# Newton steps with one operand in PSUM, and a gated half normalised by two engines, in a two-layer mixer block on one Trainium2 core

## The chip, the cores and the metric

The kernel runs on one core of one Trainium2 chip, as one launch. The metric is the device time of an execution in microseconds (us). The names used throughout are those of the profile: PE is TensorE, DVE is VectorE, ACT is ScalarE, POOL is GpSimd and SP is SyncE, which issues the loads. PSUM is the memory that PE writes its results to; SBUF is the large on-chip memory that every engine works from.

## The reference

Two layers over 512 tokens (`x`) and 256 context tokens (`ctx`), 1024 features, float32. Layer 0 mixes tokens with a gated MLP over chunks of 128 tokens beside a differential attention of four heads; layer 1 with a sliding-window attention with sinks, for the 512 tokens alone. Each layer ends with a SwiGLU feed-forward of width 2816, and a last root-mean-square norm follows.

```python
def rmsnorm(x, g):
    y = x * rsqrt(mean(x * x, axis=-1) + EPS)
    return y * g

def modulate(x, g, shift, scale):
    return rmsnorm(x, g) * (1 + scale) + shift

def chunk_mlp(u, v, w_s, b_s):          # the gated half
    u, vf = gelu(u), gelu(v)            # split in chunks of 128 tokens and 4 groups of 128 features
    mu = mean(vf, axis=-1)
    vf = (vf - mu) * rsqrt(mean((vf - mu)**2, axis=-1) + EPS)
    mixed = einsum('gpq,bnqgc->bnpgc', w_s, vf) + b_s
    return u * mixed

def diff_attn(q, k, v, lam):
    p = softmax(q @ k * scale)          # two maps for each head
    return (p[0] - lam * p[1]) @ v

# layer 0: y = concat(chunk_mlp(u, v), rmsnorm(diff_attn(q, k, vv), subln_g) * (1 - lam_init)) @ w_out
```

## The kernel before

Activations are kept feature-major: a tile has 128 features on the partitions, and 512 + 256 = 768 tokens in its columns. A float32 product is made of three matmuls on halves (`mm3`, L99, L100, L101): each operand is split into a rounded half (a cast on ACT, L115 or L75) and a rest (a subtraction on DVE or POOL: `split` L116, `unit` L78 for weights).

The program is written with tiles and a scheduler. Before anything runs, the scheduler simulates the engines and sets the order of the instructions on each one, by priorities and its simulated times; the pools of tiles decide which instruction must wait for a buffer. On the chip each engine then works through its list in that order. A stage may be pulled ahead of others by `tc.high_priority`. PSUM has three kinds of buffers here: `bank()` (three, tag `pb` in the profile), `fill()` (one, `pf`) and `wide()` (two, `pw`).

A norm over features goes like this. `squares` gathers squares; `rstd_diag` (L138 to L171) takes them with a ones matrix (L149, more terms L153) into a bank, so that each token's sum of squares stands in a column per block of 128 tokens. L156 (or L158 in the heads, with an epsilon for each token) scales the sums and adds epsilon, from PSUM into a small SBUF tile of 2 to 6 columns (`sm`). `rsqrt_small` (L123 to L133) makes the reciprocal root: a seed on the bits (L128), and three Newton steps of three instructions each (L130, L131, L132), all in SBUF on DVE. L165 writes one diagonal matrix for each block (`ident` times the root); `spread` multiplies it with ones on PE (L175), which puts the root of each token on all partitions. Fourteen such norms are in the kernel: before the mixers and the feed-forwards, one for each of the four heads of layer 0, and the last one. `rstd_small`, used for the gated half, calls the same `rsqrt_small` on 24 columns (`sf`).

The order around the change in layer 0 is: `head(0)` to `head(3)` (attention; scores into `wide()`, maximum L534, exponential, difference L542, transposes L554 into a bank, split, product with the values into another bank). `norm(t-1, …)` for the head before is called inside `head(t)`; for the last head it follows behind it. Beside the heads PE has the input products of the gated MLP (`gated`, into `fill()`), and for each of four groups `turn` (transposes L634, copy, statistics on DVE). Then `rs = rstd_small(...)` and `mix(g, rs)` for g = 0 to 3: on a group's six blocks, in two halves of four and two, L648 normalises a block in place on DVE (subtract the mean `mv[:, t, 0:1]`, multiply by the root), L649 multiplies it with the 128 x 128 chunk matrix into `pw = self.fill()`, and L650 evacuates the half and adds the bias. L677 multiplies by the other, gelu-activated half, and a split (L115, L116) prepares the operand of the output projection, whose eight weight slabs are loaded, cast (L75) and subtracted (L78) beside it. The slabs are used in the order heads 0, 1, 2, groups 0 to 3, head 3; the rests of the second and third head's operands (`k in (5, 6)`) are made by POOL's L116.

Of the kernel before, what the change touches and what calls it, by code (L numbers as in the profile page):

```python
# [6 lines left out]
F32 = mybir.dt.float32  # L7
F32R = mybir.dt.float32r
BF16 = mybir.dt.bfloat16
I32 = mybir.dt.int32  # L10
AF = mybir.ActivationFunctionType
ALU = mybir.AluOpType
AX = mybir.AxisListType.X

P = 128
# [11 lines left out]
class Builder:  # L27
# [96 lines left out]
    def rsqrt_small(self, v, n, tag="sm", bufs=6):  # L124
# [7 lines left out]
            ve.scalar_tensor_tensor(y, t, 1.5, y, ALU.add, ALU.mult)  # L132
        return y  # L133

    def rstd_rows(self, acc, T, inv, bank=None, dg=None, more=(), out=None):
        return self.spread(self.rstd_diag([(acc, T)], inv, bank, None, dg, more)[0], out or bank)

    def rstd_diag(self, accs, inv, bank=None, eps=None, at=None, more=()):  # L138

        nc = self.nc  # L140
        nb = sum(T for _, T in accs) // P
        ms = self.small(nb)
        o = 0
        for acc, T in accs:
            ps = (bank or self.bank)()
            n = T // P
            for j in range(n):
                c = slice(j * P, (j + 1) * P)
                nc.tensor.matmul(ps[:, c], acc[:, c], self.ones, start=j == 0, stop=not more, skip_group_check=True)  # L149
            for t in more:  # L150
                for j in range(n):
                    c = slice(j * P, (j + 1) * P)
                    nc.tensor.matmul(ps[:, c], t[:, c], self.ones, start=False, stop=t is more[-1], skip_group_check=True)  # L153
            col = ps[:, 0:T].rearrange("p (j f) -> p j f", f=P)[:, :, 0]
            if eps is None:
                nc.vector.tensor_scalar(ms[:, o:o + n], col, inv, EPS, ALU.mult, ALU.add)  # L156
            else:
                nc.vector.scalar_tensor_tensor(ms[:, o:o + n], col, inv, eps[:, o:o + n], ALU.mult, ALU.add)  # L158
            o += n
        r = self.rsqrt_small(ms, nb)  # L160
        dgs, o = [], 0
        for acc, T in accs:
            dg = at if at is not None else self.tmp()
            for j in range(T // P):
                self.last_diag = nc.vector.tensor_scalar(dg[:, j * P:(j + 1) * P], self.ident, r[:, o + j:o + j + 1], None,  # L165
                                                         ALU.mult)
            dgs.append(dg[:, :T])
            o += T // P
        return dgs
# [142 lines left out]
    def even(self):  # L312
        tc, nc, a = self.tc, self.nc, self.a
# [13 lines left out]
        for k in range(0, KT, 2):  # L327
            t = self.load(Rh, a["xT"][k * P:(k + 2) * P, :].rearrange("(k p) t -> p k t", p=P), [P, 2, TX], f"hx{k}")
# [110 lines left out]
        for half, heads in enumerate(((0, 1), (2, 3))):  # L439
# [3 lines left out]
            for k in range(KT):  # L443
                t = self.adap.tile([P, 2, 512], F32R, name=self.uid("wq"), tag="wq", bufs=3) if k % 3 == 2 else None
# [8 lines left out]
                if half == 0:  # L453
                    t, sh = hx[k], self.modcol(0, 0, k, 0)
# [29 lines left out]
        Rv = tc.alloc_tile_pool(name="v0", bufs=1, side="right", reuse_waits="tile")  # L484
# [5 lines left out]
        for k in range(KT):  # L490
            W = self.unit(a["v0"][k * P:(k + 1) * P, :], 512)
            for tb in range(6):
                c = slice(tb * P, (tb + 1) * P)
# [74 lines left out]
        def gated(i):  # L568

            W = self.blocks(a["uv"][i])  # L570
            u = f3()
            for off, T, A in ((0, TX, axx), (TX, TC, axc)):
                ps = self.fill()[:, :T]
                self.dense(ps, W, A)
                nc.scalar.copy(u[:, off:off + T], ps)
            raw[i] = u
# [49 lines left out]
        mv = Rv.tile([P, 24, 2], F32, name="mv")  # L626
# [14 lines left out]
        def mix(g, rs):  # L641

            vg = raw[4 + g]
            for off, n in halves:
                pw = self.fill()
                for i in range(n):
                    s, t = slice((off + i) * P, (off + i + 1) * P), g * 6 + off + i
                    nc.vector.tensor_scalar(vg[:, s], vg[:, s], mv[:, t, 0:1], rs[:, t:t + 1], ALU.subtract, ALU.mult)  # L648
                    nc.tensor.matmul(pw[:, i * P:(i + 1) * P], vg[:, s], sguT[:, g * P:(g + 1) * P], start=True, stop=True)  # L649
                nc.vector.tensor_tensor(vg[:, off * P:(off + n) * P].rearrange("p (n q) -> p n q", q=P),  # L650
                                        pw[:, :n * P].rearrange("p (n q) -> p n q", q=P),
                                        sgub[:, g * P:(g + 1) * P].unsqueeze(1).to_broadcast([P, n, P]), ALU.add)
# [13 lines left out]
        for g in range(4):  # L666
            turn(g)
            gated(g)
        rs = self.rstd_small(mv[:, :, 1], 24, 1.0, "sf")
        for g in range(4):  # L670
            mix(g, rs)
        cat = {}
# [708 lines left out]
```

## Time and profile before

| quantity | value |
|---|---|
| median of three runs | 1652.94 us (1651.64 to 1657.9) |
| profiled execution | 1665.51 us, of which the span 1663.7 |
| busy in the span | PE 1547.9, DVE 1079.5, POOL 811.8, ACT 720.6 us |
| mean granted clock of PE | 0.97 |

The span is the time from the first to the last instruction that the profile holds. Times in the timeline are counted from its start. A line of the timeline gives the start, the duration from the start of the first to the end of the last of a run of equal instructions, engine, line, operation, the tile written and those read, shapes, the number of instructions, and in brackets the idle time of the engine before it with what ended it. Layer 0's heads run from about 180 to 325 us, the turn to its output projection lies around 320 to 350, layer 1's first norm at 973, and the last norm from 1643.

### The profile page before, as it was taken

To read this page: it belongs to the slowest core of one execution; us is meant where nothing else is said; L and a number is where in the kernel's file an instruction comes from. 1 tells how busy PE (TensorE), PEld (TensorE's weight loads), DVE (VectorE), ACT (ScalarE), POOL (GpSimd) and SP (SyncE) were. 2 spreads that over 40 slices of the span, in tenths; PEclk is the share of its full clock that TensorE was granted. 3 is DMA by queue.
4 is the path that set the end of the run, shared out by engine and by line. 5 is a ranking of instruction groups with operands and counts; after the bars stand their busy time and mean duration, and the time that the engine had idled before them with its cause. 6 is when DMAs were issued, how large, how long until landed. Compare 5 with 4: busy or idle time off the path is not lost.

```text
span 1663.7 us, 24643 instructions
## 1 busy us (share of the span) xinstructions
PE 1547.9 (93%) x9547; PEld 1372.0 (82%) x9547; DVE 1079.5 (65%) x1953; ACT 720.6 (43%) x1460; POOL 811.8 (49%) x581
## 2 busy tenths in 40 slices
PE   6999989989889998999999988999989899999996
PEld 4776867889878898999999978777869889898886
DVE  4622787855666888666667585665667756566665
ACT  2413665633443332333333244556665444444443
POOL 0562211050666756766676415532224766666662
PEclk9999989989999999999999999999999999999998
DMA  8754100123122424343342012110233132223201
GB/s 313 296 173 148 33 7 1 64 79 125 51 77 89 139 90 139 118 149 136 132 144 95 26 50 83 58 33 20 77 120 116 55 111 89 102 77 114 89 26 51
DMA packets 47957, 161.98 MB, mean 97 GB/s; under 512 B 5472, under 2 KB 9952, under 8 KB 40160
## 3 DMA queue, kind: packets, MB, share of 16 engines
q1 hardware_dynamic: 47696, 160.28, 28.1%
q8 instruction: 75, 1.23, 0.3%
q14 instruction: 42, 0.34, 0.1%
q10 hardware_dynamic: 144, 0.13, 0.0%
HBM read 158.29 MB, written 2.10 MB: 96 GB/s over the span
## 4 chain that ended last, share of the span: by engine, by line
PE 70%; DVE 14%; ACT 4%; DMA 4%; POOL 3%; issue 3%; POOLq 0%; SPq 0%; DVEq 0%; ACTq 0%
PE pw L99 9%; PE pw L100 9%; PE pw L101 9%; PE pb L99 8%; PE pb L100 8%; PE pb L101 8%; DMA raw<-ffn_in 3%; POOL w L896 3%; PE pf L99 2%; PE pf L100 2%; PE pf L101 2%; PE pb L1234 2%; PE pb L1223 2%; DVE junk L220 2%; PE pf L349 2%
## 5 line engine op out<-in xcount | busy, mean ns | idle before, releaser
L99 PE MATMUL pw<-ax,w 128*128 128x384 f32 (+2 forms) x732 | 239.4, 331 | 22.8 <-DVE hs L929 6.6
L78 POOL TENSOR_TENSOR w<-raw,w 128x512 fp32r<-128x512 f32 (+1 forms) x84 | 127.8, 1528 | 249.3 <-ACT w L75 226.6
L100 PE MATMUL pw<-ax,w 128*128 128x384 f32 (+2 forms) x732 | 240.1, 328 | 4.0 <-DVE ax L193 2.6
L101 PE MATMUL pw<-ax,w 128*128 128x384 f32 (+2 forms) x732 | 238.3, 326 | 2.2 <-POOL w L896 2.2
L896 POOL TENSOR_TENSOR w<-raw,w 128x512 fp32r<-128x512 f32 x124 | 192.2, 1565 | 43.1 <-ACT w L893 43.1
L896 POOL TENSOR_TENSOR w<-t,w 128x512 fp32r<-128x512 f32 x92 | 133.0, 1445 | 143.7 <-ACT w L893 142.1
L99 PE MATMUL pb<-hh,w 128*128 128x512 f32 x480 | 168.0, 363 | 14.2 <-ACT hh L115 8.5
L99 PEld LDWEIGHTS pw<-ax,w 128*128 128x128 f32 x732 | 143.6, 197 | 34.7 <-DVE hs L929 6.9
L100 PE MATMUL pb<-hh,w 128*128 128x512 f32 x480 | 171.1, 357 | 0.0
L101 PE MATMUL pb<-hh,w 128*128 128x512 f32 x480 | 170.9, 357 | 0.0
L99 PE MATMUL pw<-T,w 128*128 128x384 f32 (+1 forms) x508 | 158.7, 312 | 9.3 <-DVE hs L929 4.7
L757 DVE SCALAR_TENSOR_TENSOR xT<-pb,mod,xT 128x512 f32<-128x512 f32 (+3 forms) x208 | 144.4, 703 | 26.0 <-PE pb L101 25.4
L100 PE MATMUL pw<-T,w 128*128 128x384 f32 (+1 forms) x508 | 157.8, 311 | 2.1 <-DVE T L116 1.5
L101 PE MATMUL pw<-T,w 128*128 128x384 f32 (+1 forms) x508 | 157.4, 310 | 0.0
L100 PEld LDWEIGHTS pw<-ax,w 128*128 128x128 f32 x732 | 144.4, 197 | 12.1 <-DVE ax L193 3.6
L101 PEld LDWEIGHTS pw<-ax,w 128*128 128x128 f32 x732 | 144.0, 197 | 6.1 <-POOL w L896 2.6
L893 ACT CAST w<-t 128x512 fp32r<-128x512 f32 x104 | 64.5, 621 | 184.1 <-DVE t L945 139.0
L99 PEld LDWEIGHTS pb<-hh,w 128*128 128x128 f32 x480 | 89.9, 190 | 28.6 <-ACT hh L115 10.9
L99 PEld LDWEIGHTS pw<-T,w 128*128 128x128 f32 x508 | 96.6, 190 | 14.2 <-DVE hs L929 5.2
L220 DVE SCALAR_TENSOR_TENSOR junk<-ar,cb 128x1024 bf16<-128x1024 f32 x64 | 106.7, 1667 | 0.2
L896 POOL TENSOR_TENSOR w<-rawo,w 128x512 fp32r<-128x512 f32 x66 | 95.2, 1443 | 19.7 <-ACT w L893 19.7
L101 PEld LDWEIGHTS pb<-hh,w 128*128 128x128 f32 x480 | 90.5, 188 | 13.1
(364 smaller groups left out, 4077.1 us busy)
## 6 DMA issues: line engine op xcount, KB each, us to landing
raw<-ffn_in SPq DMA_DIRECT2D x44, 1024.0 KB, 5.0
ar<-ada SPq DMA_DIRECT2D x24, 1024.0 KB, 6.9
ar<-ada SPq DMA_DIRECT2D x48, 512.0 KB, 3.8
rawo<-ffn_out SPq DMA_DIRECT2D x44, 512.0 KB, 3.8
raw<-odd_out SPq DMA_DIRECT2D x32, 256.0 KB, 2.7
raw<-qk SPq DMA_DIRECT2D x16, 256.0 KB, 7.6
raw<-uv SPq DMA_DIRECT2D x16, 256.0 KB, 2.7
raw<-even_out SPq DMA_DIRECT2D x8, 512.0 KB, 3.5
```

The source lines that it names most:

```text
L78: eng.tensor_tensor(lo, raw, hi.bitcast(F32), ALU.subtract)
L99: mm(out, s[0], m[0], start=start, stop=False, **kw)
L100: mm(out, s[0], m[1], start=False, stop=False, **kw)
L101: return mm(out, s[1], m[0], start=False, stop=stop, **kw)
L220: self.nc.vector.scalar_tensor_tensor(junk, t, 1.0, self.cb[who], ALU.mult, ALU.mult, accum_out=self.acc[who][:, col:col + 1])
L349: nc.tensor.matmul(ps[32 * q:32 * q + 32, :w], cst[:, k, :], t[:, w * q:w * q + w], start=k == 0, stop=k == KT - 1, skip_group_check=True)
L757: self.nc.vector.scalar_tensor_tensor(h, ps[:, r], self.modcol(l, j, m, who), h, ALU.mult, ALU.add)
L893: nc.scalar.copy(t[:, 0, :], src)
L896: eng.tensor_tensor(t[:, 1, :], src, t[:, 0, :].bitcast(F32), ALU.subtract)
L1223: last = nc.tensor.transpose(pt[:, x * P:(x + 1) * P], es[2 * (x % 2) + x // 2][:, kb * P:(kb + 1) * P], self.ident)
L1234: nc.tensor.matmul(po[64 * h:64 * h + 64, :], V[vb][:, 64 * g:64 * g + 64], t[:, h * TC:h * TC + TC], start=kb == 0, stop=kb == nb - 1, sk ...
```

## The change

Two things are changed.

*The Newton iteration* of the fourteen norms is `rsqrt_bank`. Beside the root `y` it carries the product `x` = v·y, so that in each round `tp` = -0.5·x·y is made from both, and y = (tp + 1.5)·y and x = (t + 1.5)·x follow, `t` being a second copy of `tp` in SBUF. The value v, `x` and `tp` lie in PSUM, in columns 16, 32 and 48 of the bank that held the first sums; y and `t` lie in SBUF. So each instruction has one operand in PSUM and at most one in SBUF. It takes 12 instructions behind the scaling, where there were 10. The bank stays in use until the last of them. Where a norm has two sets of sums, both scalings write to the first bank.

*The gated half.* Blocks with an odd number are normalised by ACT, as Identity with scale `rs` and bias `mb` = -mean·`rs` (a new 24-column tile, one DVE instruction), the others by DVE as before. The second half of each group (two blocks) is mixed into a `bank()`, the first (four) into `fill()` as before.

```diff
+    def rsqrt_bank(self, v, n, x, tp):
+        ve = self.nc.vector
+        y, t = self.small(n), self.small(n)
+        ve.tensor_scalar(y.bitcast(I32), v.bitcast(I32), -0.5, float(0x5F3759DF), ALU.mult, ALU.add)
+        ve.tensor_tensor(x, v, y, ALU.mult)
+        for i in range(3):
+            ve.scalar_tensor_tensor(tp, x, -0.5, y, ALU.mult, ALU.mult)
+            if i < 2:
+                ve.scalar_tensor_tensor(t, x, -0.5, y, ALU.mult, ALU.mult)
+                ve.scalar_tensor_tensor(x, t, 1.5, x, ALU.add, ALU.mult)
+            ve.scalar_tensor_tensor(y, tp, 1.5, y, ALU.add, ALU.mult)
+        return y
...
-        ms = self.small(nb)
         o = 0
         for acc, T in accs:
             ps = (bank or self.bank)()
+            if not o:
+                ms, *at2 = [ps[:, c:c + nb] for c in (16, 32, 48)]
...
-        r = self.rsqrt_small(ms, nb)
+        r = self.rsqrt_bank(ms, nb, *at2)
...
             for off, n in halves:
-                pw = self.fill()
+                pw = (self.bank if off else self.fill)()
                 for i in range(n):
                     s, t = slice((off + i) * P, (off + i + 1) * P), g * 6 + off + i
-                    nc.vector.tensor_scalar(vg[:, s], vg[:, s], mv[:, t, 0:1], rs[:, t:t + 1], ALU.subtract, ALU.mult)
+                    if i % 2:
+                        nc.scalar.activation(vg[:, s], vg[:, s], AF.Identity, bias=mb[:, t:t + 1], scale=rs[:, t:t + 1])
+                    else:
+                        nc.vector.tensor_scalar(vg[:, s], vg[:, s], mv[:, t, 0:1], rs[:, t:t + 1], ALU.subtract, ALU.mult)
...
         rs = self.rstd_small(mv[:, :, 1], 24, 1.0, "sf")
+        mb = Rv.tile([P, 24], F32, name="mb")
+        nc.vector.scalar_tensor_tensor(mb, mv[:, :, 0], -1.0, rs, ALU.mult, ALU.mult)
```

The scheduler's order moves with it. The rows below are the program's lists in order; the line numbers of after are its own (L174 is before's L158, L181 is L165, L191 is L175, L615 is L599, L668 is L649, L669 is L650, L698 is L677; L140 to L147 are the new steps).

DVE at the turn, before, from the normalisations (`f`) on; `sm` is the last head's norm, `pf_3129` and `pf_3139` are the first mixed halves:

```order
L648 TENSOR_SCALAR f_374_2099<-f_374_2099,mv,sf_3117 128x128 x6
L158 SCALAR_TENSOR_TENSOR sm_2738<-pb_2739,sx_2457 128x4
L116 TENSOR_TENSOR ax_3194<-o_1337,ax_3193 128x768
L128 TENSOR_SCALAR sm_2749<-sm_2738 128x6
L130 TENSOR_TENSOR sm_2750<-sm_2749 128x6
L131 SCALAR_TENSOR_TENSOR sm_2750<-sm_2750,sm_2738 128x6
L132 SCALAR_TENSOR_TENSOR sm_2749<-sm_2750,sm_2749 128x6
L650 TENSOR_TENSOR f_353_1910<-pf_3129,sgub_1297 128x512
...
L165 TENSOR_SCALAR q_2761<-ident_97,sm_2749 128x128 x4
L165 TENSOR_SCALAR q_2766<-ident_97,sm_2749 128x128 x2
L650 TENSOR_TENSOR f_360_1973<-pf_3145,sgub_1297 128x512
```

DVE at the same place, after:

```order
L690 SCALAR_TENSOR_TENSOR mb<-mv,sf_3123 128x24
L667 TENSOR_SCALAR f_371_2102<-f_371_2102,mv,sf_3123 128x128 x3
L174 SCALAR_TENSOR_TENSOR pb_2743<-pb_2743,sx_2461 128x4
L140 TENSOR_SCALAR sm_2753<-pb_2743 128x6
...
L147 SCALAR_TENSOR_TENSOR sm_2753<-pb_2743,sm_2753 128x6
L181 TENSOR_SCALAR q_2767<-ident_97,sm_2753 128x128 x4
L181 TENSOR_SCALAR q_2772<-ident_97,sm_2753 128x128 x2
L116 TENSOR_TENSOR ax_3202<-o_1339,ax_3201 128x768
L615 SCALAR_TENSOR_TENSOR o_2460<-o_2460,subg_1313,pb_2775 128x512
L615 SCALAR_TENSOR_TENSOR o_2460<-o_2460,subg_1313,pb_2778 128x256
L669 TENSOR_TENSOR f_350_1913<-pb_3147,sgub_1299 128x256
```

The new `mb` stands ahead of the normalisations. No evacuation of a mixed half stands within the norm any more: the first, L669, comes behind the norm's diagonals, an L116 and both L615, which read the spread roots `pb_2775` and `pb_2778`.

PE at the turn, before; `pw_3312` and its like are the output projection:

```order
L649 MATMUL pf_3129<-sguT_1295,f_353_1910 128x128 x4
L649 MATMUL pf_3139<-sguT_1295,f_353_1910 128x128 x2
L649 MATMUL pf_3145<-sguT_1295,f_360_1973 128x128 x4
L99 MATMUL pw_3312<-ax_3193,w_3256 128x384
L100 MATMUL pw_3312<-ax_3194,w_3256 128x384
L99 MATMUL pw_3313<-ax_3193,w_3256 128x384
L100 MATMUL pw_3313<-ax_3194,w_3256 128x384
L175 MATMUL pb_2769<-q_2761,ones 128x512
L175 MATMUL pb_2772<-q_2766,ones 128x256
L101 MATMUL pw_3312<-ax_3193,w_3256 128x384
```

After:

```order
L191 MATMUL pb_2775<-q_2767,ones 128x512
L191 MATMUL pb_2778<-q_2772,ones 128x256
L668 MATMUL pb_3147<-sguT_1297,f_350_1913 128x128 x2
L668 MATMUL pf_3137<-sguT_1297,f_350_1913 128x128 x4
L668 MATMUL pb_3163<-sguT_1297,f_357_1976 128x128 x2
L668 MATMUL pb_3179<-sguT_1297,f_364_2039 128x128 x2
L668 MATMUL pb_3195<-sguT_1297,f_371_2102 128x128 x2
L668 MATMUL pf_3153<-sguT_1297,f_357_1976 128x128 x4
L99 MATMUL pw_3320<-ax_3201,w_3264 128x384
L100 MATMUL pw_3320<-ax_3202,w_3264 128x384
```

PE had three halves to mix, four matmuls of the projection and then the spread of the last head's norm. Now the spread comes first, and six of the eight halves are mixed ahead of the projection, four of them in banks.

DVE in the second head, before, at the norm of the first head (`sm_1706`, `sm_1707`); `e` and `sa` are the attention's, `atl` the rests of its transposed maps:

```order
L132 SCALAR_TENSOR_TENSOR sm_1706<-sm_1707,sm_1706 128x6
L116 TENSOR_TENSOR atl_1779<-pb_1773,ath_1778 128x512
L534 TENSOR_REDUCE sa_1862<-pw_1870 128x1
L541 SCALAR_TENSOR_TENSOR sa_1857<-sa_1857,nlam,sa_1844 128x1
L130 TENSOR_TENSOR sm_1707<-sm_1706 128x6
L543 SCALAR_TENSOR_TENSOR sx_1601<-sa_1863 128x1
L542 SCALAR_TENSOR_TENSOR e_1849<-e_1855,sa_1857,e_1849 128x256
L116 TENSOR_TENSOR atl_1794<-pb_1788,ath_1793 128x512
L131 SCALAR_TENSOR_TENSOR sm_1707<-sm_1707,sm_1695 128x6
...
L132 SCALAR_TENSOR_TENSOR sm_1706<-sm_1707,sm_1706 128x6
L165 TENSOR_SCALAR q_1718<-ident_97,sm_1706 128x128 x4
```

After; `pb_1697` is the first bank of sums, in which the steps now work:

```order
L145 SCALAR_TENSOR_TENSOR sm_1708<-pb_1697,sm_1707 128x6
L116 TENSOR_TENSOR atl_1782<-pb_1776,ath_1781 128x512
L557 SCALAR_TENSOR_TENSOR sa_1860<-sa_1860,nlam,sa_1847 128x1
L146 SCALAR_TENSOR_TENSOR pb_1697<-sm_1708,pb_1697 128x6
L558 SCALAR_TENSOR_TENSOR e_1852<-e_1858,sa_1860,e_1852 128x256
L147 SCALAR_TENSOR_TENSOR sm_1707<-pb_1697,sm_1707 128x6
...
L147 SCALAR_TENSOR_TENSOR sm_1707<-pb_1697,sm_1707 128x6
L181 TENSOR_SCALAR q_1721<-ident_97,sm_1707 128x128 x4
L181 TENSOR_SCALAR q_1726<-ident_97,sm_1707 128x128 x2
...
L116 TENSOR_TENSOR atl_1797<-pb_1791,ath_1796 128x512
```

The second rest of that stretch, `atl_1794` before, stood between two Newton steps; its counterpart `atl_1797` now stands behind the norm's diagonals.

## The prediction

> **What bounds the kernel now.** I read the page first.
>
> ```profile
> span 1663.7 us, 24643 instructions
> PE 1547.9 (93%) x9547; PEld 1372.0 (82%) x9547; DVE 1079.5 (65%) x1953; ACT 720.6 (43%) x1460; POOL 811.8 (49%) x581
> PE 70%; DVE 14%; ACT 4%; DMA 4%; POOL 3%; issue 3%; POOLq 0%; SPq 0%; DVEq 0%; ACTq 0%
> ```
> TensorE (PE) is busy 93% of the span and holds 70% of the chain that ended last; VectorE (DVE) holds 14%. A stage is worth something to this change only where PE waits, so I went through the windows for stretches with PE holes, and from these into the timelines.
>
> ```profile
> 220.00:240.00 20.00, 15.72 (x109) 13.91 (x107) 17.69 (x49) 16.23 (x32) 2.58 (x2) 0.91 0.00 1
> 240.00:260.00 20.00, 16.41 (x71) 13.13 (x72) 14.94 (x37) 12.49 (x24) 1.81 (x1) 0.83 0.01 1
> 260.00:280.00 20.00, 17.25 (x109) 15.41 (x108) 18.04 (x56) 13.73 (x30) 4.60 (x3) 0.85 0.00 1
> 320.00:340.00 20.00, 12.22 (x72) 10.54 (x72) 18.76 (x49) 7.13 (x10) 8.74 (x4) 0.88 0.51 172
> ```
> Columns: PE, PEld, DVE, ACT, POOL busy, then the granted clock. From 320 to 340 us PE is busy 12.2 of 20 us: the turn from attention to the output projection, which the change edits. From 220 to 280, in the heads, PE loses 2.8 to 4.3 us per 20, DVE is busy up to 18 and the clock is at 0.83 to 0.91. The timeline of the turn, PE, DVE, then POOL:
>
> ```profile
> 325.47 1.50 PE L149 MATMUL pb<-ones,sq 128*128 128x128 f32 x12
> 330.29 1.16 PE L649 MATMUL pf<-sguT,f 128*128 128x128 f32 x8 [0.46 <-ACT f L575]
> 338.36 1.23 PE L649 MATMUL pf<-sguT,f 128*128 128x128 f32 x4 [6.91 <-DVE f L650]
> 322.39 6.24 DVE L648 TENSOR_SCALAR f<-f,mv,sf 128x128 f32<-128x128 f32 x24
> 329.56 1.79 DVE L128 TENSOR_SCALAR sm<-sm 128x6 int32<-128x6 int32 x1
> 331.39 1.72 DVE L130 TENSOR_TENSOR sm<-sm 128x6 f32<-128x6 f32 x1
> 333.15 2.26 DVE L131 SCALAR_TENSOR_TENSOR sm<-sm,sm 128x6 f32<-128x6 f32 x1
> 335.44 2.27 DVE L132 SCALAR_TENSOR_TENSOR sm<-sm,sm 128x6 f32<-128x6 f32 x1
> 337.63 0.68 DVE L650 TENSOR_TENSOR f<-pf,sgub 128x512 f32<-128x512 f32 x1
> 341.15 1.27 DVE L165 TENSOR_SCALAR q<-ident,sm 128x128 f32<-128x128 f32 x6
> 328.95 4.14 POOL L116 TENSOR_TENSOR ax<-o,ax 128x768 fp32r<-128x768 f32 x2 [55.79 <-ACT ax L115]
> 333.05 4.63 POOL L78 TENSOR_TENSOR w<-raw,w 128x1024 fp32r<-128x1024 f32 x2
> ```
> PE ran one group of mixing matmuls at 330.29 and stood still for 6.91 us, until DVE's evacuation L650, queued behind four Newton steps on a 128x6 tile. Each of these took 1.7 to 2.3 us and ended with one of POOL's four instructions (two L116, two L78, back to back to 337.68). All the same steps together:
>
> ```profile
> L130 DVE TENSOR_TENSOR sm<-sm x42: 143/161/1724, 14.4 to 1653.6; 128x2 f32<-128x2 f32 x18, 128x6 f32<-128x6 f32 x12, 128x4 f32<-128x4 f32 x6, 128x3 f32<-128x3 f32 x6
> L156 DVE TENSOR_SCALAR sm<-pb x5: 145/159/163, 14.0 to 1271.4; 128x2 f32<-128x2 f32 x3, 128x4 f32<-128x4 f32 x1, 128x3 f32<-128x3 f32 x1
> 354.80 0.68 DVE L650 TENSOR_TENSOR f<-pf,sgub 128x512 f32<-128x512 f32 x1
> 352.71 2.17 DVE L116 TENSOR_TENSOR ax<-f,ax 128x768 fp32r<-128x768 f32 x1 [0.90 <-ACT ax L115]
> 346.24 16.35 POOL L78 TENSOR_TENSOR w<-raw,w 128x1024 fp32r<-128x1024 f32 x6 [8.55 <-ACT w L75]
> 977.09 1.88 DVE L165 TENSOR_SCALAR q<-ident,sm 128x128 f32<-128x128 f32 x4
> ```
> A step takes 161 ns at the median and 1724 at most. L156 reads PSUM and never goes above 163 ns. While POOL ran L78 without a break from 346.24 to 362.6, L650 (one operand in PSUM) took 0.68 us, L116 (both in SBUF) 2.17. So DVE gives way to POOL when an instruction needs two SBUF reads, one DVE instruction per POOL instruction. The diagonal, L165 (ident, SBUF to SBUF), does too: four of them took 1.88 us at 977.09 as POOL's L78 began, while six took 1.27 at 341.15.
>
> **The change part by part.** The sum is made against the profiled execution: 1665.51 us, 1663.7 of span and 1.8 around it, 12.6 above the median of 1652.94; I shift by the difference.
>
> *Newton in a bank.* Every step now has one operand in PSUM and one in SBUF, so by the rows above it stops waiting for POOL. A norm has 13 short instructions for 11. Free of waits they start 0.20 us apart (337.63's neighbours and the first norm), so a norm is 0.4 us longer. No instruction of before writes PSUM from DVE; the nearest rows are the PSUM read at 159 ns and the SBUF step at 161. I take equal. The bad end is L156's own maximum of 163 ns against the minimum of L130, 143: 20 ns on each of 182 steps (13 in 14 norms), under 4 us if none lay beside other work; the good end is no difference. The Trainium skill ("Perfetto Trace Analysis", Optimizing Scalar/DVE Operations) speaks against the change here: it puts DVE's overhead per instruction at about 60 ns on SBUF and 125 on PSUM; by that a norm would be an estimated 0.8 us longer still (13 times 65 ns) and the sum some 3 us higher. The row of L156 disagrees for reads.
>
> *The turn.* Removed: four blocked steps. Moved: the evacuations L650 now stand behind the whole norm of the last head, its six diagonals, an L116 and two L599, and PE spreads the norm before it mixes. DVE's normalisations halve: 24 took 6.24 us from 322.39; 12 take 3.1, behind `mb` (0.2), to 325.7. ACT takes 12 from 322.6 on:
>
> ```profile
> L831 ACT ACTIVATE hh<-hh,mod 128x128 f32<-128x128 f32 x6 | 2.3, 390 | 0.0
> 325.72 0.58 ACT L575 COPY f<-pf 128x512 f32<-128x512 f32 x1 [4.55 <-PE pf L101]
> 327.25 2.30 ACT L115 CAST ax<-o 128x768 fp32r<-128x768 f32 x3 [0.94 <-PE pf L100]
> ```
> 390 ns each, and as ACT starts one 0.1 before the last ends (three casts of 0.83 took 2.30), 0.30 apart: 3.6 us, to 326.2. ACT's copy L575 then starts 0.5 us late, and PE, busy with L149 until 326.97, hides that but for 0.1. So DVE has the sums at 327.0, runs 13 steps and reaches the first diagonal at 329.6. POOL begins its four instructions after the second of ACT's casts L115, at 328.95, now 329.0. The diagonals are 0.6 us too late: I expect the block to move from the steps to them. One passes per POOL instruction; the fourth comes out with the last, near 337.3 (POOL's first is not held up by DVE's L116, 0.4 saved), the other two, L116 and the two L599 follow by 340.5. PE gets the spread at 337.4 instead of evacuated data at 338.36, and the clock decides the rest:
>
> ```profile
> 332.00:335.30 3.30, 0.00 (x0) 0.00 (x0) 3.27 (x2) 1.00 (x2) 3.30 (x2) 1.00 0.00 0
> 338.70:342.10 3.40, 2.88 (x13) 2.59 (x13) 2.69 (x11) 1.01 (x2) 0.00 (x0) 0.50 0.43 152
> 342.10:345.50 3.40, 3.40 (x10) 2.28 (x8) 2.08 (x5) 3.39 (x4) 0.00 (x0) 0.50 0.00 0
> 348.64 0.60 PE L649 MATMUL pf<-sguT,f 128*128 128x128 f32 x4
> 353.10 1.05 PE L649 MATMUL pf<-sguT,f 128*128 128x128 f32 x8
> ```
> The clock fell to 0.50 after a stretch without matmuls, and came back only after 3.4 us in which PE was busy throughout (2.88 of 3.40 wasn't enough). Before, PE entered the projection (P from here) at 345.46 with four of its matmuls done (0.7 us) and five mixing groups owed (28 matmuls; eight took 1.05 and four 0.60 at full clock, so each adds 0.11: 3.1): it would have ended both at 347.9 + P. With banks of both kinds PE has mixing for all of the recovery, so I expect full speed at 342.1 and the projection at 344.4 to 344.9 with two groups of eight owed (1.8): 346.2 to 346.7 + P. That is 1.2 to 1.7 earlier; I take **-1.4**. Bounds: +1 if the clock stays at half to 345.5, -10 if the block goes.
>
> *The heads.* Three norms run between the attention of the next head. DVE is the fullest engine there (18.04 of 20), so 2 x 0.2 x 3 = 1.2 us. And the first bank of sums, freed before by its first read, is held to the last step:
>
> ```profile
> 226.51 0.16 DVE L158 SCALAR_TENSOR_TENSOR sm<-pb,sx 128x4 f32<-128x4 f32 x1 [0.40 <-PE pb L149]
> 238.95 1.27 DVE L165 TENSOR_SCALAR q<-ident,sm 128x128 f32<-128x128 f32 x6
> ```
> Now it is held from 226.5 to the last step just ahead of 238.95, one bank of three, while the next head's transposes L554 need banks too. In the new order the second set of them comes behind the norm, and its cast on ACT (0.58 us for 512 columns, as L575 above) behind the gelus. I take **+1.8**: the three norms and one cast. Bounds: -1, since the order changes and PE has filler, and +11 (below).
>
> *The middle norm* (973 to 987) has a blocked L130 and L131 in the second half's chain, between modulations that PE waits for; two steps more in the first. The diagonal there ends with POOL's L78 anyway, which hides them. **-0.5**, from +0.4 to -1.5.
>
> *The last norm:*
>
> ```profile
> 1651.53 0.68 DVE L130 TENSOR_TENSOR sm<-sm 128x2 f32<-128x2 f32 x1
> 1654.29 0.65 DVE L131 SCALAR_TENSOR_TENSOR sm<-sm,sm 128x2 f32<-128x2 f32 x1
> 1655.16 0.48 DVE L165 TENSOR_SCALAR dg<-ident,sm 128x128 f32<-128x128 f32 x2
> 1650.78 4.14 POOL L1301 TENSOR_TENSOR xT<-xT,rs 128x256 f32<-128x256 f32 x6 [3.28 <-ACT rs L1291]
> 1655.70 1.22 PE L175 MATMUL pf<-dg,ones 128*128 128x256 f32 x2 [5.41 <-DVE dg L165]
> ```
> Five steps waited for POOL's six multiplications. Now 13 steps and L1303 take from 1649.8 to 1653.3; the half before is 0.4 later, since two more steps follow its last L757. The two diagonals wait for POOL once each: done by 1654.7 instead of 1655.6. Nothing hides PE's spread, so **-0.9** (0 to -1.5). The remaining norms lie under PE's work; if that cover were gone, 0.4 each for five, 2 us.
>
> Sum: -1.4 + 1.8 - 0.5 - 0.9 = -1.0 us. 1664.5 in a profiled run, 1652.0 by the median.
>
> **The rivals.** *Bank starvation, slower.* The held bank stalls the attention itself. Price: each of three holds delays a set of transposes by a cycle of transposes, cast and subtraction (0.6 for four matmuls, half of the eight's 1.16, then 0.58 and 0.68 as the rows of L575 and L650: 1.9 us) and starves PE long enough for one more 3.4 us at half clock (1.7): 3.6, three times 11; with the other terms, +8.5: 1661.5. It decides where PE has no filler (mixing inputs of L99) between the stalls. For: clock and holes of 240 to 260 above. Against: the filler is there, and the order puts it there.
>
> *The block goes, faster.* If the diagonals pass before POOL's run, PE's 6.9 us hole closes, and the half-clock work after it (2.88 + 3.40 us at half, 3.1 lost) with it: -10 in the turn; with +1.8, -0.5 and -0.9, -9.6: 1643.5. It needs 0.6 us: a Newton step faster than 0.15 us, or casts later by that. Against: steps have never been under 143 ns, and ACT's 12 delay the casts by 0.1 only. The Trainium skill ("SBUF — State Buffer", Who interferes with whom) has `tensor_scalar` able to take the shared ports in its two-port modes; by that the diagonals wait, as L165 at 977.09 does.
>
> *The change doesn't do what it says.* If steps with one operand in PSUM wait too (a write, not a read, taking the port), the last steps and then the diagonals are blocked: +2 in the turn, +1.5 at the end, about 1657. Against: L650 beside L116.
>
> **How the numbers follow.** Forecast 0.69, starvation 0.13, block gone 0.14, no effect 0.04. A measurement of this kernel can tell about 0.5% (8.3 us) from no change; the forecast's terms by themselves lie within that, as does the third rival. So faster 0.14, same 0.73, slower 0.13. The range reaches from the block gone, 1643.5, to 1661, just short of full starvation; the bounds of the single terms (one or two heads stalled, the clock late, the steps 20 ns longer) lie inside.
>
> **What would show it.** Right: the short steps in a bank stay near 0.16 us beside POOL, at 1650 too; six diagonals behind the last head's norm take 6 to 9 us, ended by POOL; PE's hole of 329.6 to 337 stays; the last diagonal ends near 1654.7. Wrong: diagonals of 1.3 us there and PE mixing by 332; PSUM steps above 0.2 us; new holes of PE with half clock in 225 to 310; the turn more than 3 us off in either direction.

## The result, and the profile after

The changed kernel takes 1661.39 us (median of 16 runs, 1657.06 to 1668.61) against 1654.3 us of the kernel before (16 runs, 1650.67 to 1657.9): ratio 1.0049, 95% interval 1.0036 to 1.0062: some 8 us slower by the ratio, 7.1 by the medians. The forecast was 1652 with a range to 1661.

The profiled execution of before that the prediction used (1665.51 us) was a long one, 11 us above its runs' median, while that of after (span 1659.8) is near its median. The two pages set side by side would show a gain. A second and a third profile of before have spans of 1653.4 and 1648.6 us; they are what after is compared with here. The head of the page of after:

```profile
span 1659.8 us, 24676 instructions
PE 1548.3 (93%) x9547; PEld 1373.4 (83%) x9547; DVE 1076.7 (65%) x1970; ACT 723.7 (44%) x1472; POOL 810.5 (49%) x581
PE 71%; DVE 12%; POOL 4%; ACT 4%; DMA 4%; issue 4%; POOLq 0%; SPq 0%; ACTq 0%; DVEq 0%
```
PE's share of the chain rose from 70 to 71%, POOL's from 3 to 4, DVE's fell from 14 to 12: averages that don't tell the place. So I cut each profile at the same matmuls. Stage times in us, worked out from the starts of matched matmuls in the timelines: *heads* from the first sums of the first head's norm to those of the last head's, *turn* from there to a matmul of the output projection (384 us), then the feed-forward of layer 0 to 960, layer 1's first norms and inputs to 1085, attention to 1190, attention's end, output projection, norms and the first products of the feed-forward to 1393 (*layer 1*), the rest to 1622, and *last* with the last norm (the bounds are named by their times in the second profile of before).

| profile | heads | turn | to 960 | to 1085 | to 1190 | layer 1 | to 1622 | last | span |
|---|---|---|---|---|---|---|---|---|---|
| before, second | 96.4 | 62.1 | 575.9 | 125.0 | 105.1 | 202.9 | 229.2 | 31.2 | 1653.4 |
| before, third | 96.6 | 62.2 | 574.2 | 124.3 | 105.1 | 200.3 | 228.9 | 31.2 | 1648.6 |
| before, first | 100.0 | 63.2 | 580.3 | 125.0 | 105.1 | 202.6 | 230.7 | 31.3 | 1663.7 |
| after | 103.5 | 59.9 | 575.6 | 123.1 | 105.1 | 207.4 | 230.4 | 30.0 | 1659.8 |
| after, second | 103.5 | 59.5 | 577.8 | 123.5 | 105.1 | 207.2 | 229.2 | 30.0 | 1662.6 |

The turn and the last norm gain 2.4 and 1.2 us. The heads lose 7 (3.5 against the one long profile of before), and layer 1 loses 4.4 to 7, in a stretch where the change touches two short norms. The stages to 960 and to 1622 vary by 2 to 6 us between profiles of one kernel; nothing is read from them.

**The turn.** The timeline of after, ACT, DVE, POOL, then PE (L665 is ACT's normalisation, L174 the scaled sums, L181 the diagonals, L191 the spread, L668 the mixing):

```profile
325.53 4.73 ACT L665 ACTIVATE f<-f,mb,sf 128x128 f32<-128x128 f32 x12 [1.43 <-DVE mb L690]
331.32 2.30 ACT L115 CAST ax<-o 128x768 fp32r<-128x768 f32 x3 [0.59 <-PE pf L100]
329.90 0.17 DVE L174 SCALAR_TENSOR_TENSOR pb<-pb,sx 128x2 f32<-128x2 f32 x1 [0.28 <-PE pb L165]
332.53 6.52 DVE L181 TENSOR_SCALAR q<-ident,sm 128x128 f32<-128x128 f32 x6
338.97 3.12 DVE L116 TENSOR_TENSOR ax<-o,ax 128x768 fp32r<-128x768 f32 x1
333.02 3.65 POOL L116 TENSOR_TENSOR ax<-o,ax 128x768 fp32r<-128x768 f32 x2 [57.85 <-ACT ax L115]
336.63 4.65 POOL L78 TENSOR_TENSOR w<-raw,w 128x1024 fp32r<-128x1024 f32 x2
335.03 1.12 PE L191 MATMUL pb<-q,ones 128*128 128x512 f32 x2 [1.13 <-DVE q L181]
339.20 1.19 PE L191 MATMUL pb<-q,ones 128*128 128x256 f32 x2 [3.04 <-DVE q L181]
```
ACT's twelve normalisations took 4.73 us, 0.39 apart, where 3.6 was forecast; the casts began at 331.32, and so POOL's run at 333.02. The steps ran free of POOL, 0.20 apart, and DVE reached the first diagonal at 332.53, half a microsecond ahead of POOL. Three diagonals passed, the other three waited for one POOL instruction each (6.52 us for all, 1.27 where nothing blocks), and the L116 behind them for a fourth. The block did move from the steps to the diagonals, and PE's one hole of 6.9 us became two of 1.1 and 3.0. By the clock records of the traces the half clock lasted 6.8 us there, two windows of 3.41, where before it lasted 10.2, three. The turn goes by this number in all eighteen profiles of this document: 62.0 to 63.2 us with three windows, 59.5 to 59.9 with two, 57.6 with one, and 56.3 to 56.4 with none (e2, p2, q6 and r3 below).

**The steps.** Three kinds of steps in the nine norms whose sums lie in a bank `pb`, minimum, median and maximum in ns:

```profile
L140 DVE TENSOR_SCALAR sm<-pb x9: 145/155/164, 14.2 to 1270.7; 128x6 int32<-128x6 int32 x4, 128x2 int32<-128x2 int32 x3, 128x4 int32<-128x4 int32 x1, 128x3 int32<-128x3 int32 x1
L143 DVE SCALAR_TENSOR_TENSOR pb<-pb,sm x27: 154/170/173, 14.6 to 1273.1; 128x6 f32<-128x6 f32 x12, 128x2 f32<-128x2 f32 x9, 128x4 f32<-128x4 f32 x3, 128x3 f32<-128x3 f32 x3
L147 DVE SCALAR_TENSOR_TENSOR sm<-pb,sm x27: 147/160/166, 15.2 to 1273.3; 128x6 f32<-128x6 f32 x12, 128x2 f32<-128x2 f32 x9, 128x4 f32<-128x4 f32 x3, 128x3 f32<-128x3 f32 x3
```
170 ns where PSUM is read and written, 155 to 160 where it is only read. No step of any of the fourteen norms is above 173, beside POOL too.

**The last norm**, DVE, POOL and PE:

```profile
1650.18 0.16 DVE L147 SCALAR_TENSOR_TENSOR sm<-pw,sm 128x2 f32<-128x2 f32 x1
1650.38 1.42 DVE L181 TENSOR_SCALAR dg<-ident,sm 128x128 f32<-128x128 f32 x2
1648.26 4.13 POOL L1322 TENSOR_TENSOR xT<-xT,rs 128x256 f32<-128x256 f32 x6 [3.42 <-ACT rs L1312]
1651.85 1.14 PE L191 MATMUL pf<-dg,ones 128*128 128x256 f32 x2 [4.07 <-DVE dg L181]
```
No step waits any more. The two diagonals take 1.42 us beside POOL, and PE's spread starts at 1651.85, 3.6 us after POOL's start at 1648.26; before it was 4.9 (1655.70 after 1650.78).

**Layer 1.** PE's wait for the rest of one weight block, in after:

```profile
1239.41 0.58 PE L101 MATMUL pb<-ax,w 128*128 128x256 f32 x1 [2.12 <-DVE w L78]
```
and in p2_mix_pinned (below), where this stretch has the issue order of before:

```profile
1232.47 0.39 PE L101 MATMUL pb<-ax,w 128*128 128x256 f32 x1 [0.89 <-DVE w L78]
```
This one wait is 1.2 us longer, so it is a part of the loss and not the whole.

### The profile page after: what moved, and what is told of

It reads as the page before. It is cut to its first block, busy times and chain, and to the rows that moved or that the text cites. A ratio compares the mean times of both kernels' runs of the same rounds, so it can differ in the third digit from the quotient of the medians.

```text
span 1659.8 us, 24676 instructions
## 1 busy us (share of the span) xinstructions
PE 1548.3 (93%) x9547; PEld 1373.4 (83%) x9547; DVE 1076.7 (65%) x1970; ACT 723.7 (44%) x1472; POOL 810.5 (49%) x581
## 4 chain that ended last, share of the span: by engine, by line
PE 71%; DVE 12%; POOL 4%; ACT 4%; DMA 4%; issue 4%; POOLq 0%; SPq 0%; ACTq 0%; DVEq 0%
PE pw L99 9%; PE pw L100 9%; PE pw L101 9%; PE pb L99 8%; PE pb L100 8%; PE pb L101 8%; POOL w L917 3%; PE pf L99 2%; DMA raw<-ffn_in 2%; PE pf L100 2%; PE pb L1255 2%; PE pf L101 2%; PE pb L1244 2%; PE pf L365 2%; DVE junk L236 1%
## 5 line engine op out<-in xcount | busy, mean ns | idle before, releaser
L101 PE MATMUL pw<-ax,w 128*128 128x384 f32 (+2 forms) x732 | 237.2, 326 | 2.2 <-POOL w L917 2.2
L101 PE MATMUL pb<-hh,w 128*128 128x512 f32 x480 | 170.9, 357 | 0.0
L101 PE MATMUL pw<-T,w 128*128 128x384 f32 (+1 forms) x508 | 157.8, 311 | 0.0
L101 PEld LDWEIGHTS pw<-ax,w 128*128 128x128 f32 x732 | 143.4, 196 | 5.7 <-POOL w L917 2.6
L99 PEld LDWEIGHTS pb<-hh,w 128*128 128x128 f32 x480 | 89.6, 189 | 25.0 <-ACT hh L115 10.5
L99 PEld LDWEIGHTS pw<-T,w 128*128 128x128 f32 x508 | 97.0, 191 | 12.9 <-DVE hs L950 5.2
L100 PEld LDWEIGHTS pw<-T,w 128*128 128x128 f32 x508 | 96.9, 191 | 5.6 <-DVE T L116 3.2
```

The costliest lines, as they stand in the source:

```text
L99: mm(out, s[0], m[0], start=start, stop=False, **kw)
L100: mm(out, s[0], m[1], start=False, stop=False, **kw)
L101: return mm(out, s[1], m[0], start=False, stop=stop, **kw)
```

## The experiments

Two theories were set against each other after the traces: that the new instructions cost the time where they stand (more steps, a bank that is held), and that the scheduler's new order costs it, of instructions that the change does not touch.

**One part alone.** e1_newton_only leaves the gated half as before; e2_mix_only leaves `rsqrt_small`. Against after, one line of each (ACT's normalisation and `mb` go in e1 too):

```diff
e1: -                pw = (self.bank if off else self.fill)()
e1: +                pw = self.fill()
e2: -        r = self.rsqrt_bank(ms, nb, *at2)
e2: +        r = self.rsqrt_small(ms, nb)
```

> The Newton steps in a bank for all fourteen norms, the gated half as before. Theory A (the loss sits in layer 1, 1205 to 1345 us, behind norms whose steps stand in PSUM and whose buffer is held to the last step): +5 to +8 us against before, and the matmuls of that stretch fall behind by some 5 to 7 us. Theory B (the loss comes from the gated half's change, by what the scheduler moves with it): 0 to -2 us here. Theory C (the time of the two kernels differs by chance of the loads): within 2 us of before, with no fixed place.

Measured: 1659.38 us, ratio 1.0032 [1.0019, 1.0045]. Heads 103.6, turn 57.6, layer 1 205.3, last 29.9.

> The gated half by two engines and two kinds of banks, Newton as before. Theory A: within 2 us of before, or faster if the evacuations leave the Newton chain. Theory B: +6 to +8 us. Theory C: within 2 us.

Measured: 1653.53 us, ratio 0.9995 [0.998, 1.001]. Heads 96.9, turn 56.4, layer 1 207.1, last 31.3.

By the totals theory A comes out in both runs, by the stages it does not: it put e1's loss into layer 1, where 2.4 to 5 us of it lie, and had no loss there for e2. So it is the new Newton steps that bring the heads their 7 us. The mixing alone gains 5.7 us in the turn and loses it again some 900 us later: layer 1 takes 207 us in a kernel whose layer 1 has not one instruction changed. The turn of e2, DVE, POOL, PE (L165 diagonals, L175 spread):

```profile
325.27 0.16 DVE L158 SCALAR_TENSOR_TENSOR sm<-pb,sx 128x2 f32<-128x2 f32 x1 [0.28 <-PE pb L149]
327.48 2.85 DVE L165 TENSOR_SCALAR q<-ident,sm 128x128 f32<-128x128 f32 x6
328.36 3.66 POOL L116 TENSOR_TENSOR ax<-o,ax 128x768 fp32r<-128x768 f32 x2 [54.00 <-DVE q L165]
330.47 0.67 PE L175 MATMUL pb<-q,ones 128*128 128x256 f32 x2 [0.37 <-DVE q L165]
```
There the diagonals begin 2.21 us after the sums (L158 at 325.27), five of six before POOL starts. In after it is 2.63 (329.90 to 332.53): two steps at 0.20. These 0.4 us let POOL take two more places in the row: from the first diagonal to the end of L116 after takes 9.6 us and e2 5.4 (L116 ends at 342.09 and 332.83). The parts gain 5.7 and 4.5 us alone, 2.4 together.

> The kernel before, for a second profile. If the profiled execution of before (1665.5 us) was a slow one, this one is 8 to 14 us shorter, and the places where the two profiles of one kernel part show which stretches vary by chance. Theory A: layer 1 from 1205 to 1345 takes the same here as in the first profile within 2 us. Theory C: it differs by 5 us or more.

> The changed kernel again, for a second profile: +7 to +9 us against before. Theory A: heads +3.4, turn -3.3 and layer 1 from 1205 to 1345 +7 us against before, as in the first pair of profiles. Theory C: the places change.

Measured: e3 1655.18 us in one run; e4 1663.3 us, ratio 1.0059 [1.0041, 1.0077]. Their stages are in the table: in e4 heads and layer 1 come back to 0.2 us, so the theory of chance falls for these two.

**The order of layer 1.** The build numbers its instructions in the order in which the code issues them, and those of layer 1 are the same in before and e2 but for a shift of two. A list of these numbers holds each engine to a given order, by edges that add no wait. PE in that stretch, before, then e2 (`pw_11921` and `pw_11923` are the same tile):

```order
L100 MATMUL pb_11707<-ax_11523,w_11715 128x256
L101 MATMUL pw_11921<-ax_11554,w_11911 128x256
L99 MATMUL pw_11921<-ax_11559,w_11911 128x256
L100 MATMUL pw_11921<-ax_11559,w_11911 128x256
L101 MATMUL pw_11921<-ax_11559,w_11911 128x256
L99 MATMUL pw_11921<-ax_11564,w_11911 128x256
L101 MATMUL pb_11707<-ax_11523,w_11715 128x256
```
```order
L100 MATMUL pb_11709<-ax_11525,w_11717 128x256
L101 MATMUL pb_11709<-ax_11525,w_11717 128x256
...
L101 MATMUL pb_11709<-ax_11534,w_11717 128x256
L101 MATMUL pw_11923<-ax_11556,w_11913 128x256
```
Before, five matmuls of another tile cover the time until the rest of `w_11715` is there (L101 reads it). The new order puts them behind. The function that holds an order, shortened:

```diff
+def pin(tc, shift):
+    here = {i.name: i for i in tc.nc.cur_bb.bb.instructions}
+    kind = mybir.DependencyInfo(mybir.DependencyClass.NoSync, mybir.DependencyReason.DATA)
+    for steps in PIN:
...
+                tc.add_manual_dep(ins, last.name, kind, reason="pin")
```

> The kernel before, every instruction unchanged, but with the issue order of layer 1's stretch (odd attention's end, output projection, first products of the feed-forward) that the scheduler gave to the kernel with the gated half changed. Theory O (what layer 1 loses is the order alone): +4 us against before, all of it between 1190 and 1375 us. Rival (layer 1 loses because layer 0 ends in another state, loads or clock): 0 +- 1 us.

Measured: 1659.05 us, ratio 1.004 [1.0025, 1.0056]; layer 1 207.3, every stage up to 1190 as in e3 within 0.2.

> The gated half changed, Newton as before, with layer 1's stretch held to the issue order of before. Theory O: -4 to -5.5 us against before (the gain of the turn stays, the loss of layer 1 goes). Rival: -1 us, as without the held order.

Measured: 1647.24 us, ratio 0.9961 [0.9945, 0.9976]; turn 56.4, layer 1 203.0. Theory O holds both ways; p2's gain of 6.8 us is larger than forecast. In all, layer 1 takes 199.6 to 203.0 us in the eleven profiles with its old order, and 204.8 to 207.4 in the seven with the new one. In q5 below the new steps themselves run there, in the old order, and it takes 201.0. Three windows of e3_before_again, then of p1:

```profile
1230.00:1250.00 20.00, 18.60 (x149) 17.79 (x148) 14.79 (x24) 11.01 (x26) 7.67 (x7) 1.00 0.62 222
1290.00:1310.00 20.00, 16.82 (x99) 15.27 (x100) 15.46 (x22) 9.37 (x20) 15.96 (x13) 0.91 0.27 88
1330.00:1350.00 20.00, 20.00 (x133) 18.26 (x132) 14.87 (x21) 7.59 (x16) 13.76 (x10) 1.00 0.24 80
```
```profile
1230.00:1250.00 20.00, 17.86 (x132) 17.25 (x132) 13.57 (x21) 9.69 (x24) 7.18 (x7) 0.91 0.57 198
1290.00:1310.00 20.00, 15.35 (x92) 14.48 (x91) 16.02 (x25) 10.21 (x23) 13.41 (x12) 0.83 0.16 52
1330.00:1350.00 20.00, 18.49 (x123) 16.81 (x122) 15.05 (x23) 8.23 (x16) 13.43 (x9) 1.00 0.32 118
```
Same instructions, same inputs: PE is busy 0.7 to 1.5 us less in each, and the granted clock is 0.91 for 1.00 and 0.83 for 0.91 in the first two. These are the three with the largest losses; over all eight from 1190 to 1350, one of which gains 0.9, PE is busy 144.1 us for 147.4, 3.3 less.

**The heads.** h1 puts only the last Newton product into the first bank of sums, in the heads; h2 runs the twelve steps with all operands in SBUF.

```diff
h1: +            if i == 2 and held is not None:
h1: +                t = held
h2: -        r = self.rsqrt_small(ms, nb)
h2: +        r = self.rsqrt_small(ms, nb) if eps is None else self.rsqrt_bank(ms, nb, self.small(nb, "nx", 2), self.small(nb, "nx", 2))
```

> Before, with one change: in the four heads' norms the last Newton step puts its product in the first bank of sums, so that this bank is held to the last step; ten steps in number as before. Theory H (the held bank costs the heads): heads (190 to 312 us) +5 to +7 us, and with layer 1's order, which may move too, +8 us or more in all. Theory S (more steps cost the heads): heads within 1 us of before.

> Before, with one change: in the four heads' norms the twelve new Newton steps, all operands in SBUF, no bank held. Theory H: heads within 2 us of before. Theory S: heads +5 to +7 us. Either: the turn is no faster than before, since steps in SBUF still wait for POOL.

Measured: h1 1664.97 us, ratio 1.0066 [1.0051, 1.0082], heads 101.3, layer 1 207.2; h2 1660.37 us, ratio 1.0044 [1.003, 1.0059], heads 101.8, layer 1 204.8. Each of them alone costs the heads 5 us, and each has a new order in the heads and in layer 1: neither theory had that. The expectation that h2's turn would be no faster missed too: it took 59.6 us against 62.1, and PE's hole there is 4.8 us and not 6.9. So order and bank were separated. q1 is before, every instruction unchanged, in h1's order of layer 0; q4 is h1 in the order of before. The code is that of `pin`, with other lists.

> The kernel before, every instruction unchanged and no bank held, in the issue order that the held bank of h1_hold gave to layer 0, and layer 1 in the order of before. Theory O2 (the heads lose by the order alone): last head's sums 4 to 5.5 us later than before, counted from the first head's sums, and +4 to +6 us in all. Theory H (the wait for the held bank itself): heads within 1 us of before.

> The held bank of h1_hold, with every engine in the issue order of before. Theory O2: within 1.5 us of before in the heads and in all. Theory H: heads +4 us or more, since the next transposes then wait for the bank in place.

Measured: q1 1656.18 us, ratio 1.0033 [1.0023, 1.0043], heads 103.3; q4 1654.37 us, ratio 1.0022 [1.0006, 1.0038], heads 100.7. The order alone, with no bank held, makes the heads as long as in after; h1's order of PE there is nearly that of after, not quite the same. Windows of before (third profile), then of q1:

```profile
265.00:285.00 20.00, 17.26 (x109) 14.80 (x108) 18.90 (x60) 12.41 (x28) 3.30 (x2) 1.00 0.00 1
285.00:305.00 20.00, 19.85 (x138) 17.91 (x137) 18.01 (x63) 14.41 (x32) 0.00 (x0) 1.00 0.01 2
305.00:325.00 20.00, 18.99 (x122) 16.34 (x122) 13.43 (x52) 7.79 (x15) 0.00 (x0) 1.00 0.35 122
```
```profile
265.00:285.00 20.00, 17.80 (x98) 14.86 (x97) 17.32 (x56) 10.70 (x24) 3.58 (x3) 0.91 0.00 1
285.00:305.00 20.00, 18.35 (x122) 16.79 (x121) 16.13 (x48) 11.70 (x27) 0.00 (x0) 0.91 0.00 1
305.00:325.00 20.00, 17.66 (x108) 14.74 (x107) 11.81 (x49) 10.28 (x19) 0.00 (x0) 1.00 0.09 27
```
From 285 on PE is busy 1.3 to 1.5 us less in 20. Over the whole of the heads the mean granted clock is 0.90 in q1 and in both profiles of after, against 0.91, 0.96 and 0.95 in the three of before. One of its new waits, in the timeline of q1, is for the rest of a transposed map (`atl`), which DVE now writes later:

```profile
271.74 0.58 PE L100 MATMUL pb<-atl,vhi 128*128 128x256 f32 x1 [1.15 <-DVE atl L116]
```

The heads of q4 could be chance, since before took 100.0 in its first profile too. More profiles of the same order settle it:

> q4_hold_pinned again, for a second profile. If the held bank costs the heads by itself: 100 to 101 us from the first to the last head's sums, as in the first. If chance: 96.4 or 100.

> q4_hold_pinned a third time. If the held bank costs the heads by itself: 100 to 101 us again. If chance: 96.4 or 100.

> Before, a third profile: 96.4 or 100 us from the first to the last head's sums.

Measured: heads 100.1 in r1, 100.2 in r2, 96.6 in r4 (one run each, 1656.17, 1655.93 and 1650.38 us). With a held bank and PE's order of before, four profiles of four (q5 below among them) take 100.0 to 100.7; without, six of eight take 96.4 to 96.9 and two 99.9 and 100.0. q4's twelve runs are 3.5 us longer by the median. So the bank costs some 3 us by itself where the order is kept. In q4 the transposes wait until another bank has been emptied, by ACT's copy `o` and by DVE's L116; in before (second profile, last two lines) they follow without a wait:

```profile
271.65 0.65 PE L558 MATMUL pb<-ident,e 128*128 128x128 f32 x4 [1.42 <-ACT o L570]
275.26 1.12 PE L558 MATMUL pb<-ident,e 128*128 128x128 f32 x4 [1.87 <-DVE atl L116]
269.27 0.60 PE L554 MATMUL pb<-ident,e 128*128 128x128 f32 x4
272.43 0.60 PE L554 MATMUL pb<-ident,e 128*128 128x128 f32 x4
```
The two costs do not add: 103.3 us with the order alone (q1), 101.3 with the same order and the held bank (h1), 103.5 with both in after. These are single profiles. h1 loses its 5 us at a mean granted clock of 0.97, so the half clock is not the only way in which this order costs time, and the 2 us between them are not explained.

**All of the change in the old order.**

> The changed kernel, all its instructions, with those that it shares with p2_mix_pinned held to that kernel's order; the Newton steps are free. If order made the whole loss: -4 to -7 us against before (heads 0 to +1, turn -2 to -5, layer 1 0, middle and last norm -2). If the two steps more or the held bank cost the heads in themselves: -1 to +3 us.

Measured: 1648.81 us, ratio 0.9987 [0.9975, 0.9998]; heads 100.0, turn 59.5, layer 1 201.0, last 30.0. The changed kernel, with not one instruction changed, is 0.6% faster in another order, and then 2 us faster than before: less than expected. Of the heads' 7 us the old order gives back 3.5 (103.5 to 100.0); the other 3.5 stay with the held bank, and the two steps more add nothing to be seen, since q4, r1 and r2 with ten steps take 100.1 to 100.7. The turn takes 59.5 and not the 56.4 of p2, which has the same order and shorter steps: so the 0.4 us of steps cost 3.1 there, and two windows at half clock come with it.

**The parts that gain.** q6 is p2 with the new steps in layer 1's first norms and the last norm only.

```diff
+        self.in_bank = True
         r = self.rstd_rows(sq[:, off:off + n], n, 1.0 / D, self.wide, dg, more, self.bank if off else self.fill)
+        self.in_bank = False
```

> p2_mix_pinned with the new Newton steps in the bank for layer 1's first norms and the last norm only, where they stood beside POOL, and the shared instructions held to p2_mix_pinned's order: 1 us less in 967 to 992, 1.2 us less at the end, -8 to -9 us against before, about 1645.5. If the steps in a bank gain nothing there: -6 us, as p2_mix_pinned.

> q6_best again: 96.4 or 100 us in the heads, by chance; -8 +- 2 us against before.

Measured: q6 1642.38 us, ratio 0.9946 [0.9929, 0.9962]; r3 1644.59 us, ratio 0.9953 [0.9934, 0.9971]. Turn 56.4 and 56.3, last 30.1, heads 99.9 and 96.5. It beats both kernels. What the new steps add to p2 (0.9961 [0.9945, 0.9976]) is not clear of the noise in the totals; in the last stage it is 1.3 us.

## Why the prediction was wrong

- *Newton in a bank.* Right. Steps of 160 to 170 ns beside POOL too, 0.20 us apart; those that write PSUM take 9 ns more than the old ones (170 against 161), within the bad end of 20. "1724 at most" for the old steps was L130's alone; L131 and L132 reached 2.26 us, as the timeline had shown. The Trainium skill ("Perfetto Trace Analysis", Optimizing Scalar/DVE Operations) gives an overhead of about 125 ns on PSUM and 60 on SBUF; a row 65 ns longer does not show here.
- *The turn*, forecast -1.4, measured -2.2 to -2.7. The mechanism was right, the block moved to the diagonals, and one size was off: ACT's normalisations are 0.39 us apart, not 0.30, which delayed the casts and POOL more than DVE (POOL starts 3.2 us after PE's sums end, 333.02 after 329.87, where before it was 2.0), and so three diagonals passed, where none was expected. That it "needs 0.6 us" for the block to go was the right scale: e2, 0.4 us shorter, gains 5.7.
- *The heads*, forecast +1.8, measured +7: the step that failed. It counted instructions on DVE and one cast, and took the new order as harmless: "the filler is there, and the order puts it there". The order was not harmless: 103.3 us without any bank held (q1), and after in the old order is 3.5 us shorter (q5). The other 3.5 are the held bank. That the new order takes the filler away from PE is the reading of its waits, not a separate test. The sign named for being wrong, new holes of PE with half clock in 225 to 310, is the one that came: 20.5 us of after's heads are at half clock, against 6.8 and 10.2 in the second and third profile of before.
- *The remaining norms* "lie under PE's work", costed at nothing: the second step that failed, 4.4 us or more in layer 1. The norms do lie under it (q5: 201.0 us with the new steps). What changed there was the order of matmuls that the change does not touch, and I had priced instructions, not order. p1 shows it.
- *The rival of bank starvation* named 1661.5 and 1661.39 came, by luck. Its terms add up to +8.2, not +8.5 (11 - 1.4 - 0.5 - 0.9). It had 11 us in the heads from the bank alone, where the bank makes some 3, and nothing in layer 1. The parts measured are 7 + 4.4 - 2.4 - 1.2 = 7.8 us, half of the 7 and all of the 4.4 by order.
- *The middle norm*, -0.5: 123.1 and 123.5 in the stage to 1085 against 124.3 to 125.0, but kernels with old steps there (q1, q4) also reach 123.1 to 123.4, so its share is not settled. *The last norm*, -0.9: -1.2, right.
- *The base.* The sum was shifted from a profile to the median, as if the long profile were long everywhere alike. Its heads were the long outcome (100.0 us, 96.4 and 96.6 in the others); the sum used its windows as the usual state.

## What to carry to other kernels

Where a scheduler sets the order, a local edit is two changes: its instructions, and a new order of others, here up to 900 us further on. Compare the orders engine by engine, and test the second by holding the old one with order edges: here that turned a loss of 8 us into a gain of 2, and the edit's best part into a gain of 8 to 9. Work that must finish before another engine starts a run that blocks it has a cliff, not a slope: 0.4 us of extra steps cost 3 us of the turn.

## What the runs showed of the hardware

One and the same program gave two outcomes in the heads: q6 took 99.9 us there and r3 96.5, as before took 100.0 in its first profile and 96.4 and 96.6 in the others. One window of q6, then of r3:

```profile
265.00:285.00 20.00, 17.23 (x97) 14.86 (x96) 16.87 (x56) 10.63 (x24) 3.35 (x2) 0.83 0.00 1
```
```profile
265.00:285.00 20.00, 17.25 (x109) 14.82 (x108) 18.97 (x59) 12.31 (x28) 3.32 (x2) 1.00 0.00 1
```
PE is busy the same 17.2 us in both; the granted clock is 0.83 and 1.00. Of 20 us that is 3.4 us of full-speed work, the whole difference. In the clock records of all eighteen profiles a stretch at half clock lasts 3.41 us or a whole multiple of it (but for the last of each, at the end of the span). The heads of q6 hold five such windows, 17.1 us, and those of r3 three, 10.2 us: two windows more, each at a cost of half its length, 1.7 us. The count does not explain every profile: before took 96.4 and 96.6 us with two and three of them. The Trainium skill ("TensorE: Matmul & The Clock Gate", Part 1) has the clock decided in a free-running window of about 3.4 us, which one and the same kernel meets differently from run to run. The traces agree.

The place of these windows goes with the outcome. Counted from the first sums of the heads, half clock begins a whole number of windows plus 0.5 and 0.7 us later in the two long profiles (q6 and the first of before), and plus 1.6 to 3.0 us in the six short ones that have PE's order of before and no bank held. No run sets that place, so this is seen and not tested. The four profiles with the held bank lie at 2.7 to 2.9, where the short ones lie, so their 100 us are not this chance.
